# Hybrid encoder layer: from the second pair of row tiles on, the input is also loaded laid out by columns, and row factors are spread by two transposes and multiplied in place

## The chip, the core and the metric

The kernel runs on one core of one Trainium2 chip. The metric is the device time of one execution in microseconds (us). The engines are TensorE (PE; weight loads are shown apart as PEld), VectorE (DVE), ScalarE (ACT), GpSimd (POOL) and SyncE (SP), which issues most of the DMAs.

## The reference

One encoder layer is applied to two sequences (s = 0, 1) of 1024 rows by 1024 columns, all in float32. The part that matters here is the beginning:

```python
def rmsnorm(x, g):
    xf = x.astype(jnp.float32)
    y = xf * lax.rsqrt(jnp.mean(xf * xf, axis=-1, keepdims=True) + EPS)
    return (y * g.astype(jnp.float32)).astype(x.dtype)
...
    h = rmsnorm(x, g_mix) * (1.0 + sc1) + sh1
    z = h @ w_in
    q_lat, kv_lat, k_pe, f_in = z[..., :o1], z[..., o1:o2], z[..., o2:o3], z[..., o3:]
    y_mla = mla_group(q_lat, kv_lat, k_pe, g_q_lat, w_uq, g_kv_lat, w_ukv)
    y_four = fourier_group(f_in, w_four)
    mix = jnp.concatenate([y_mla, y_four], axis=-1) @ w_out
    x = x + ga1 * mix
    ...
```

Each row of x is divided by its root mean square (the row factor r), each column is scaled by g_mix (1 + sc1) and shifted by sh1, and the result is multiplied by w_in. Attention, a Fourier mixing, an output projection and a SwiGLU feed-forward follow; the change does not touch them.

## The kernel before

The first stage works on eight pairs of row tiles, four to a sequence; `pairs[k]` is (s, j), and the two tiles u = 0, 1 of pair k are 128 rows each, one from the first half of the sequence and one from the second. Matmuls that must be exact use a high and a low part of each operand: `split` makes the high part on ACT (line 62) and the rest on DVE (line 63), and `mm3` issues three matmuls (lines 78 to 80).

For pair k these steps exist:

- `x_load(k)` loads the two tiles, 128 rows by 1024 columns each, into two of four buffers `xt` (two DMAs on SP, line 356).
- `norm(k)` squares the rows on ACT with the sum beside it (line 366), makes r with six small POOL instructions in `rstd` (lines 103 to 110; the same helper also serves the projected latents), and multiplies the rows by r in place on DVE (line 369).
- `flip(k, g)`, for g = 0 to 3, transposes four blocks of 128 x 128 on PE into one PSUM bank (line 382); ACT scales and shifts them by column into `hf`, which holds the columns on partitions (line 385), and `split` makes `hh` and `hl` of them.
- `zproj(k, u)` projects one tile (24 matmuls of 448 columns with `wz`), squares the projected latents on ACT (lines 409, 410), gets their factors from POOL, scales on DVE (lines 421, 422) and writes `kv` by DMA (line 427). `latents(k, u)` transposes the scaled latents on PE (line 436), splits them (`lh`, `ll`) and writes them by DMA (line 441).
- `evenodd(k, i)` adds (i = 0) or subtracts (i = 1) the two tiles of `hf` on POOL (line 396) and splits the result; `fourier_in(k, i)` multiplies it by `wcs` (24 matmuls of 280 or 256 columns).

`pair(k)` strings them together, with the flips of pair k+1 and the norm of pair k+2 in between. A generator `extras` puts other work at three places of a pair: eight blocks of modulation products (`mod_mm`, line 217, four matmuls each, whose 1 MB weights go through two buffers `wada`, line 208), and later products with `lw` (line 311). In pair 0 four matmuls of line 252 stand there. A scheduler then orders the instructions of each engine by its own estimate; on the chip each engine runs its list in that order and waits at semaphores. PSUM has eight banks, all handed out in turn by `bank()`. Pair 7 runs in the next stage's pool, and after it the Fourier sums, attention and feed-forward follow.

Before the first pair, modulation and weight preparation share buffers with the stage: the tag `hf` serves for two weight loads before `hf` of pair 0 is made.

Of the kernel before, what the change touches and what calls it, by code (L numbers as in the profile page):

```python
# [12 lines left out]
F32 = mybir.dt.float32  # L13
# [3 lines left out]
ALU = mybir.AluOpType  # L17
# [4 lines left out]
P = 128  # L22
D = 1024
N = 1024
NC = D // P
# [27 lines left out]
def hybrid_encoder_kernel(ctx: ExitStack, tc: tile.TileContext, a: dict):  # L53
    nc = tc.nc
# [31 lines left out]
    ident = const.tile([P, P], F32, name="ident")  # L86
# [9 lines left out]
    def rstd(ms, n, rest=None):  # L96

        v = tiny.tile([P, 2], F32, name="rs_v")[:, :n]
        y = tiny.tile([P, 2], F32, name="rs_y")[:, :n]
        w = tiny.tile([P, 2], F32, name="rs_w")[:, :n]  # L100
        r = tiny.tile([P, 2], F32, name="rs_r")[:, :n]
        if rest is None:
            nc.gpsimd.tensor_scalar(out=v, in0=ms, scalar1=EPS, scalar2=None, op0=ALU.add)
        else:
            nc.gpsimd.tensor_tensor(out=v, in0=ms, in1=rest, op=ALU.add)
        nc.gpsimd.tensor_tensor(out=y, in0=v, in1=mhalf[:, :n], op=ALU.pow)  # L106
        nc.gpsimd.tensor_tensor(out=w, in0=y, in1=y, op=ALU.mult)
        nc.gpsimd.tensor_tensor(out=w, in0=w, in1=v, op=ALU.mult)
        nc.gpsimd.tensor_scalar(out=w, in0=w, scalar1=-0.5, scalar2=1.5, op0=ALU.mult, op1=ALU.add)
        here["p"] = nc.gpsimd.tensor_tensor(out=r, in0=w, in1=y, op=ALU.mult).ins  # L110
        return r
# [52 lines left out]
    with ExitStack() as st:  # L164
        p1b = st.enter_context(ExitStack())
        w2 = p1b.enter_context(tc.tile_pool(name="p1b", bufs=1, side="right", reuse_waits="tile"))
# [3 lines left out]
        def bank():  # L170
            return pp.tile([P, 512], F32, tag="b", name="bank")

        def xtile():
            return w2.tile([P, D], F32, tag="x", name="xt", bufs=4)

        def stile(name):
            return w.tile([P, 512], F32, tag="sk", name=name, bufs=3)
# [152 lines left out]
        def wz_split(i, t):  # L330
            for b in range(0, 4, 2):
                split(wz_h[:, i + b : i + b + 2, :], wz_l[:, i + b : i + b + 2, :], t[:, b : b + 2, :])
# [17 lines left out]
        st1 = {}  # L350

        def x_load(k):
            s, j = pairs[k]
            st1["x", k] = [xtile() for _ in range(2)]
            for u in range(2):
                nc.sync.dma_start(st1["x", k][u], xs[s][rows(j, u), :])

        def norm(k):
            if ("x", k) not in st1:
                x_load(k)  # L360
            ms = tiny.tile([P, 2], F32, name="ms")
            xt = st1["x", k]
            for u in range(2):
                t = xt[u]
                jk = w.tile([P, D], BF16, tag="junk", name="junk", bufs=1)
                nc.scalar.activation(jk, t, AF.Square, scale=1.0 / 32.0, accum_out=ms[:, u : u + 1])
            r = rstd(ms, 2)
            for u in range(2):
                nc.vector.tensor_scalar(out=xt[u], in0=xt[u], scalar1=r[:, u : u + 1], scalar2=None, op0=ALU.mult)

        def flip(k, g):
            s, j = pairs[k]
            if g == 0:
                st1["hf", k] = w2.tile([P, NC, 2, P], F32, tag="hf", name="hf", bufs=1)
                st1["hh", k] = w.tile([P, NC, 2, P], F32R, tag=f"hh{k % 2}", name="hh")
                st1["hl", k] = w.tile([P, NC, 2, P], F32R, tag=f"hl{k % 2}", name="hl")
            hf, xt = st1["hf", k], st1["x", k]
            pt = bank().rearrange("p (c u t) -> p c u t", c=2, u=2)
            for c in range(2):
                for u in range(2):  # L380
                    cc = 2 * g + c
                    nc.tensor.transpose(pt[:, c, u, :], xt[u][:, cc * P : (cc + 1) * P], ident)
            for c in range(2):
                cc = 2 * g + c
                nc.scalar.activation(hf[:, cc], pt[:, c], AF.Identity, bias=sh1[s][:, cc : cc + 1], scale=s1[s][:, cc : cc + 1])
            gs = slice(2 * g, 2 * g + 2)
            split(st1["hh", k][:, gs], st1["hl", k][:, gs], hf[:, gs])

        def evenodd(k, i):
            hf = st1["hf", k] if i == 0 else st1.pop(("hf", k))  # L390
            f = w.tile([P, NC, P], F32, tag="eo", name="eo", bufs=1)
            fh = w.tile([P, NC, P], F32R, tag=f"eoh{i}", name="eoh", bufs=1)
            fl = w.tile([P, NC, P], F32R, tag=f"eol{i}", name="eol", bufs=1)
            for g in range(2):
                gs = slice(4 * g, 4 * g + 4)
                nc.gpsimd.tensor_tensor(out=f[:, gs], in0=hf[:, gs, 0, :], in1=hf[:, gs, 1, :], op=(ALU.add, ALU.subtract)[i])
                split(fh[:, gs], fl[:, gs], f[:, gs])
            st1["eo", k, i] = (fh, fl)
# [74 lines left out]
                nc.sync.dma_start(zo[1], zo[0][2:3, :])  # L473

        def wide(tag, shape=(P, 4, 512)):
            return (w2 if tag == "hf" else w).tile(list(shape), F32, tag=tag, name="wide")

        cols0 = [(0, 2048)]
        fq = fold_loads()
# [35 lines left out]
        for g in range(4):  # L515
            flip(0, g)
        wz_split(4, wz1)
        norm(1)
        nc.sync.dma_start(ropec, a["ropec"])
        nc.sync.dma_start(ropes, a["ropes"])  # L520
# [1 line left out]
            prep_wcs(i, wf[i // 4])  # L522
        zproj(0, 0)
        evenodd(0, 0)
        evenodd(0, 1)
        nk = len(pairs)
        more = extras()

        def pair(k, also=None):
            if k + 2 < nk:  # L530
                x_load(k + 2)
            if also is not None:
                also(0)
            if k > 0:
                zproj(k, 0)
            if also is not None:
                with tc.issue_after(here["sq"]):
                    also(1)
            if k + 1 < nk:
                flip(k + 1, 0)  # L540
                flip(k + 1, 1)
            next(more, None)
            zproj(k, 1)
            if k < nk - 1:
                latents(k, 0)
            if k + 1 < nk:
                flip(k + 1, 2)
                flip(k + 1, 3)
            if k + 2 < nk:
                norm(k + 2)  # L550
            next(more, None)
            fourier_in(k, 0)
            if k > 0:
                if k == nk - 1:
                    latents(k, 0)
                latents(k, 1)
            if k + 1 < nk:
                evenodd(k + 1, 0)
            next(more, None)
            fourier_in(k, 1)  # L560
            if k == 0:
                latents(k, 1)
            if k + 1 < nk:
                evenodd(k + 1, 1)

        for k in range(nk - 1):
            pair(k)
# [422 lines left out]
    with ExitStack() as st:  # L990
# [105 lines left out]
        for k in range(nit + 4):  # L1096
# [7 lines left out]
            if k < nit:  # L1104
                s, b, h, u = items[k]
# [623 lines left out]
def _layout(i):  # L1729
    slots = _slots()  # L1730
    sq = {k: np.asarray(v)[0] for k, v in i.items() if k != "g_final"}
    c = np.stack([sq["c_prompt"], sq["c_sample"]])
    w_in, w_uq, w_ukv, w4 = sq["w_in"], sq["w_uq"], sq["w_ukv"], sq["w_four"]
    uq = w_uq.reshape(QL, HEADS, NOPE + ROPE)
    ukv = w_ukv.reshape(KVL, HEADS, NOPE + VD)
    rev = (GD - np.arange(GD)) % GD
    w4t = np.stack([w4, w4[:, rev, :]], 1).transpose(0, 3, 1, 2).reshape(4, P, 2, GD).transpose(1, 0, 2, 3)
    b = sq["b_ada"]
    bga = np.zeros((P, 512), b.dtype)
    for s in range(2):  # L1740
        for j, o in enumerate((2 * D, 2 * D + 512, 5 * D, 5 * D + 512)):
            bga[32 * j + s] = b[o : o + 512]
    wgu = np.stack([sq["w_gate"], sq["w_up"]]).reshape(2, NC, P, NF, P).transpose(0, 3, 2, 1, 4)
    r = {
        "x0": sq["x_prompt"][slots], "x1": sq["x_sample"][slots],
        "cT": c.reshape(2, NC, P).transpose(2, 1, 0),
        "w_ada": sq["w_ada"], "bT": b.reshape(48, P).T, "bga": bga,
        "gT": np.stack([sq["g_mix"], sq["g_ffn"]]).reshape(2, NC, P).transpose(2, 0, 1),
        "wz": w_in[:, :DZ].reshape(NC, P, DZ).transpose(1, 0, 2),
        "wfT": w_in[:, DZ:].T.reshape(4, P, D).transpose(1, 0, 2),  # L1750
        "wuqT": uq[:, :, :NOPE].transpose(2, 1, 0),
        "wpe": uq[:, :, NOPE:].reshape(2, P, HEADS * ROPE).transpose(1, 0, 2),
        "wukT": ukv[:, :, :NOPE].transpose(2, 1, 0),
        "wuvT": ukv[:, :, NOPE:].transpose(2, 1, 0),
        "gq": np.concatenate([sq["g_q_lat"].reshape(2, P).T, sq["g_kv_lat"].reshape(KVL, 1)], 1), "gkvr": sq["g_kv_lat"],
        "w4": w4t, "w_out": sq["w_out"], "wgu": wgu, "w_down": sq["w_down"], "g_final": np.asarray(i["g_final"]),
    }
    return {k: np.ascontiguousarray(v) for k, v in r.items()}
# [19 lines left out]
```

## Time and profile before

| | before |
|---|---|
| median of 3 runs | 2047.81 us (2044.94 to 2049.38) |
| the profiled execution | 2042.28 us |
| its span, first to last instruction | 2040.5 us |
| mean granted TensorE clock | 0.992 |
| busy: PE, PEld, DVE, ACT, POOL | 97%, 80%, 69%, 44%, 41% |
| DMA moved | 370.30 MB, mean 181 GB/s |

Times in the rows are those of the one profiled execution, counted from its first instruction. Matmuls overlap, and the end of each is modelled, so the time that a group of matmuls holds PE is read from its start to the start of the next group. The share in brackets behind an instruction, where there is one, is the engine's idle time in front of it and what ended it.

### The profile page before, as it was taken

How to read it: one execution, taken by the hardware profiler on the slowest of the kernel's cores; microseconds unless marked ns; L12 is line 12 of the kernel's file. 1: busy time of each engine (PE TensorE's matmuls, PEld its weight loads, DVE VectorE, ACT ScalarE, POOL GpSimd, SP SyncE). 2: the span in 40 equal slices, each digit the busy share in tenths (PEclk: the TensorE clock that was granted, in tenths of full speed). 3: DMA queues.
4: the chain of work that ended last, by engine and by line, in shares of the span. 5: the costliest groups of instructions: out<-in, count | busy, mean ns of one | idle time of the engine just before them, and what ended most of it. 6: DMA issues, size and time to landing. Idle time of an engine off the chain costs nothing.

```text
span 2040.5 us, 27843 instructions
## 1 busy us (share of the span) xinstructions
PE 1982.0 (97%) x9610; PEld 1626.2 (80%) x9610; DVE 1407.8 (69%) x2082; ACT 897.3 (44%) x1745; POOL 835.7 (41%) x1026
## 2 busy tenths in 40 slices
PE   5999999999999999999999999999999999999997
PEld 2788877888888877888888888877788888888876
DVE  2667757766677669878777676677756666667674
ACT  2656635555465554333333365453333333336451
POOL 1455213111313317879779410332654454410142
PEclk7999999999999999999999999999999999999999
DMA  9685694544643475545655587674422322358662
GB/s 369 204 269 187 217 338 136 130 103 99 165 115 121 127 276 198 191 166 200 198 163 196 174 305 251 214 236 144 141 104 103 106 101 103 107 183 275 227 229 85
DMA packets 182505, 370.30 MB, mean 181 GB/s; under 512 B 18972, under 2 KB 58396, under 8 KB 179292
## 3 DMA queue, kind: packets, MB, share of 16 engines
q1 hardware_dynamic: 163228, 308.88, 45.2%
q0 software_dynamic: 19136, 59.65, 9.7%
q8 instruction: 75, 1.23, 0.2%
q14 instruction: 66, 0.54, 0.1%
HBM read 256.46 MB, written 120.39 MB: 185 GB/s over the span
## 4 chain that ended last, share of the span: by engine, by line
PE 54%; DVE 2%; DMA 2%; POOL 1%; issue 1%; ACT 1%; SPq 0%; DVEq 0%; ACTq 0%; POOLq 0%
PE bank L78 18%; PE bank L79 18%; PE bank L80 18%; DVE wl L63 1%; DMA draw<-s_d 1%; DMA draw<-t_d 1%; DMA val<-x_d 1%; DVE val L138 0%; ACT wh L62 0%; POOL val L138 0%; DVE val L1577 0%; DMA rgu<-in_wgu_dram 0%; POOL rs_y L106 0%; SPq L1537 0%; DVE val L135 0%
## 5 line engine op out<-in xcount | busy, mean ns | idle before, releaser
L78 PE MATMUL bank<-H,wh 128*128 128x512 f32 x1224 | 477.2, 390 | 6.5 <-DVE val L138 6.0
L80 PE MATMUL bank<-H,wl 128*128 128x512 f32 x1224 | 476.4, 389 | 0.2
L79 PE MATMUL bank<-H,wh 128*128 128x512 f32 x1224 | 476.2, 389 | 0.0
L138 DVE TENSOR_TENSOR val<-bank,val 128x512 f32<-128x512 f32 x244 | 166.7, 688 | 160.6 <-PE bank L80 156.3
L78 PEld LDWEIGHTS bank<-H,wh 128*128 128x128 f32 x1224 | 229.7, 188 | 56.8 <-DVE val L138 6.6
L80 PEld LDWEIGHTS bank<-H,wl 128*128 128x128 f32 x1224 | 229.7, 188 | 49.6 <-DVE wl L63 1.4
L79 PEld LDWEIGHTS bank<-H,wh 128*128 128x128 f32 x1224 | 229.8, 188 | 47.4
L63 DVE TENSOR_TENSOR wl<-draw,wh 128x512 fp32r<-128x512 f32 x286 | 201.4, 738 | 86.8 <-ACT wh L62 86.4
L62 ACT CAST wh<-draw 128x512 fp32r<-128x512 f32 x286 | 169.0, 620 | 158.5 <-PE bank L79 93.1
L79 PE MATMUL bank<-wl,wh 128*128 128x512 f32 x572 | 223.9, 391 | 2.7 <-DVE wl L63 2.7
L138 POOL TENSOR_TENSOR val<-val 128x512 f32<-128x512 f32 x58 | 84.4, 1462 | 343.4 <-DVE val L1551 187.0
L80 PE MATMUL bank<-wh,wl 128*128 128x512 f32 x572 | 222.7, 389 | 0.0
L78 PE MATMUL bank<-wh 128*128 128x512 f32 x572 | 222.6, 389 | 0.0
L62 ACT CAST wh<-rgu 128x512 fp32r<-128x512 f32 x171 | 106.3, 623 | 249.9 <-PE bank L79 195.4
L63 DVE TENSOR_TENSOR wl<-val,wh 128x512 fp32r<-128x512 f32 x133 | 145.2, 1093 | 72.1 <-ACT wh L62 71.8
L63 DVE TENSOR_TENSOR wl<-rgu,wh 128x512 fp32r<-128x512 f32 x171 | 168.0, 983 | 7.0 <-ACT wh L62 7.0
L62 ACT CAST wh<-val 128x512 fp32r<-128x512 f32 x133 | 82.3, 622 | 179.9 <-PE bank L79 154.1
L135 POOL TENSOR_TENSOR val<-rgu 128x512 f32<-128x512 f32 x80 | 112.8, 1411 | 96.7 <-DMA rgu<-in_wgu_dram 93.0
L79 PEld LDWEIGHTS bank<-wl,wh 128*128 128x128 f32 x572 | 107.3, 188 | 28.9 <-DVE wl L63 6.6
L78 PEld LDWEIGHTS bank<-wh 128*128 128x128 f32 x572 | 107.4, 188 | 22.4
L80 PEld LDWEIGHTS bank<-wh,wl 128*128 128x128 f32 x572 | 107.4, 188 | 22.0
L135 POOL TENSOR_TENSOR val<-val 128x512 f32<-128x512 f32 x89 | 119.3, 1359 | 1.3
(385 smaller groups left out, 3901.2 us busy)
## 6 DMA issues: line engine op xcount, KB each, us to landing
rgu<-in_wgu_dram SPq DMA_DIRECT2D x86, 512.0 KB
draw<-s_d SPq DMA_DIRECT2D x143, 256.0 KB
s_d<-val POOLq DMA_DIRECT2D x88, 256.0 KB, 3.8
draw<-t_d SPq DMA_DIRECT2D x88, 256.0 KB
s_d<-val SPq DMA_DIRECT2D x66, 256.0 KB
draw<-in_w_down_dram SPq DMA_DIRECT2D x55, 256.0 KB
wada<-in_w_ada_dram SPq DMA_DIRECT2D x13, 1024.0 KB
xt<-in_x_dram SPq DMA_DIRECT2D x16, 512.0 KB
```

The lines of the kernel that those rows point to most:

```text
L62: here["a"] = nc.scalar.copy(hi, src).ins
L63: here["v"] = nc.vector.tensor_tensor(out=lo, in0=src, in1=rd(hi), op=ALU.subtract).ins
L78: nc.tensor.matmul(out, lh, rh, start=first, stop=False, skip_group_check=cont)
L79: nc.tensor.matmul(out, lh, rl, start=False, stop=False, skip_group_check=cont)
L80: nc.tensor.matmul(out, ll, rh, start=False, stop=last, skip_group_check=cont)
L135: return eng.tensor_tensor(out=out, in0=x, in1=y, op=ALU.subtract).ins
L138: return eng.tensor_tensor(out=out, in0=x, in1=y, op=ALU.add).ins
```

## The change

The tiles are also stored in HBM a second time, transposed: `xT0` and `xT1` hold, for each j, the columns on partitions, as `hf` does (8 KB in a row on each of 128 partitions). From pair 1 on, `xT_load(k)` loads 1 MB of this straight into `hf`, which now has two buffers; `xt` has two in place of four. `norm(k)` stops at r. A new step `scale_cols(k)` transposes r, broadcast along the free axis, once for each tile, so that each partition of a PSUM bank holds the factors of all 256 rows, and DVE multiplies `hf` by it in place, in two instructions. `flip(k, g)` then has no transposes: ACT reads `hf` and writes `hf`. Pair 0 stays as it was.

```diff
@@ xtile
-            return w2.tile([P, D], F32, tag="x", name="xt", bufs=4)
+            return w2.tile([P, D], F32, tag="x", name="xt", bufs=2)
@@ behind x_load
+        def xT_load(k):
+            s, j = pairs[k]
+            st1["hf", k] = w2.tile([P, NC, 2, P], F32, tag="hf", name="hf", bufs=2)
+            nc.sync.dma_start(st1["hf", k], a[f"xT{s}"][j])
+
@@ norm
             r = rstd(ms, 2)
+            if k > 0:
+                st1["r", k] = r
+                return
             for u in range(2):
                 nc.vector.tensor_scalar(out=xt[u], in0=xt[u], scalar1=r[:, u : u + 1], scalar2=None, op0=ALU.mult)
+
+        def scale_cols(k):
+            hf, r = st1["hf", k], st1.pop(("r", k))
+            pr = bank()[:, :256].rearrange("p (u t) -> p u t", u=2)
+            for u in range(2):
+                nc.tensor.transpose(pr[:, u, :], r[:, u : u + 1].broadcast_to([P, P]), ident)
+            for g in range(2):
+                gs = slice(4 * g, 4 * g + 4)
+                nc.vector.tensor_tensor(out=hf[:, gs], in0=hf[:, gs], in1=pr.unsqueeze(1).broadcast_to([P, 4, 2, P]), op=ALU.mult)
@@ flip
             if g == 0:
-                st1["hf", k] = w2.tile([P, NC, 2, P], F32, tag="hf", name="hf", bufs=1)
+                if k == 0:
+                    st1["hf", k] = w2.tile([P, NC, 2, P], F32, tag="hf", name="hf", bufs=2)
...
-            pt = bank().rearrange("p (c u t) -> p c u t", c=2, u=2)
-            for c in range(2):
-                for u in range(2):
-                    cc = 2 * g + c
-                    nc.tensor.transpose(pt[:, c, u, :], xt[u][:, cc * P : (cc + 1) * P], ident)
+            if k > 0:
+                pt = hf[:, 2 * g : 2 * g + 2]
+            else:
+                pt = bank().rearrange("p (c u t) -> p c u t", c=2, u=2)
+                for c in range(2):
+                    for u in range(2):
+                        cc = 2 * g + c
+                        nc.tensor.transpose(pt[:, c, u, :], xt[u][:, cc * P : (cc + 1) * P], ident)
@@ before pair 0
         wz_split(4, wz1)
+        xT_load(1)
         norm(1)
...
         evenodd(0, 0)
+        scale_cols(1)
         evenodd(0, 1)
@@ pair(k)
             if k + 2 < nk:
                 x_load(k + 2)
+                xT_load(k + 2)
...
             if k + 1 < nk:
                 evenodd(k + 1, 1)
+            if k + 2 < nk:
+                scale_cols(k + 2)
@@ _layout
+        **{f"xT{s}": x[slots].reshape(2, 4, P, NC, P).transpose(1, 4, 3, 0, 2)
+           for s, x in enumerate((sq["x_prompt"], sq["x_sample"]))},
```

In the changed kernel the squares of `norm` have line 371, the multiply of pair 0 line 377, the transposes of r line 383, the multiply of `hf` line 386, the transposes of pair 0 line 403, the scaling line 406, the copies to `kv` go out at line 448 and the latents at line 462.

PE, behind the second projection of pair 0 (the last two rows of that projection come first; `lat` are the scaled latents, line 252 is the work with `wo2`). Before:

```order
L79 MATMUL bank<-wz_l,hh 128x448
L80 MATMUL bank<-wz_h,hl 128x448
L436 MATMUL bank<-ident,lat 128x128 x4
L382 MATMUL bank<-ident,xt 128x128 x8
L252 MATMUL bank<-wada,wuvT 128x512 x2
L78 MATMUL bank<-wcs_h,eoh 128x280
```

Now:

```order
L79 MATMUL bank<-wz_l,hh 128x448
L80 MATMUL bank<-wz_h,hl 128x448
L457 MATMUL bank<-ident,lat 128x128 x4
L252 MATMUL bank<-wada,wuvT 128x512 x2
L78 MATMUL bank<-wcs_h,eoh 128x280
```

The eight transposes of two flips are gone. At the end of pair 0, between the second Fourier product and the first projection of pair 1, PE has now (`rs_r` is r of pair 2; before, the fourth row was not there):

```order
L79 MATMUL bank<-wcs_l,eoh 128x256
L80 MATMUL bank<-wcs_h,eol 128x256
L457 MATMUL bank<-ident,lat 128x128 x4
L383 MATMUL bank<-ident,rs_r 128x128 x2
L78 MATMUL bank<-wz_h,hh 128x448
```

The transposes of r stand ahead of the projections of the next pair, here and in pairs 1 to 5.

ACT, in pair 1 behind its second projection (`mz` are the squares of the latents, `ms` those of pair 3's rows). Before:

```order
L409 ACTIVATE junk,mz<-bank 128x256
L410 ACTIVATE junk,mz<-bank 128x128
L62 CAST lh<-bank 128x512
L385 ACTIVATE hf<-bank,sh_0_77,s_0_75 128x256 x3
L62 CAST hh<-hf 128x512
L62 CAST kv<-lat 128x128
L385 ACTIVATE hf<-bank,sh_0_77,s_0_75 128x256
L366 ACTIVATE junk,ms<-xt 128x1024
L62 CAST hh<-hf 128x512
L366 ACTIVATE junk,ms<-xt 128x1024
```

Now:

```order
L430 ACTIVATE junk,mz<-bank 128x256
L431 ACTIVATE junk,mz<-bank 128x128
L62 CAST lh<-bank 128x512
L62 CAST hh<-hf 128x512
L371 ACTIVATE junk,ms<-xt 128x1024
L62 CAST kv<-lat 128x128
L371 ACTIVATE junk,ms<-xt 128x1024
```

The scalings of `hf` have moved ahead of the projection's end, and the first square stands ahead of the copy of `kv`.

SP, the load of the second block of modulation weights (the row with `wada` x2). Before:

```order
L427 DMA ckv_d_96<-kv 128x128
L441 DMA lat_d_93<-ll 512x1x128
L427 DMA ckv_d_97<-kv 128x128
L255 DMA wo_d<-so 128x512 x2
L208 DMA wada<-in_w_ada_dram 128x1024 x2
L441 DMA lat_d_92<-lh 512x1x128
```

Now:

```order
L462 DMA lat_d_92<-lh 512x1x128
L462 DMA lat_d_93<-ll 512x1x128
L356 DMA xt<-in_x_dram 128x1024
L361 DMA hf<-in_xT_dram 128x2048
L448 DMA ckv_d_96<-kv 128x128
L448 DMA ckv_d_97<-kv 128x128
L208 DMA wada<-in_w_ada_dram 128x1024 x2
```

The block's load was issued behind the writes of pair 0; now it stands behind the loads of pair 3 and the write of pair 1's first `kv`.

4 lines of the change are left out of this document (3 added, 1 removed).

## The prediction

> **What bounds the kernel now.** I read the page first, then busy time in stretches cut at the pairs of row tiles, then TensorE (PE) in order of time, and last the waits.
>
> ```profile
> PE 1982.0 (97%) x9610; PEld 1626.2 (80%) x9610; DVE 1407.8 (69%) x2082; ACT 897.3 (44%) x1745; POOL 835.7 (41%) x1026
> ```
>
> PE is busy nearly all the time, so only PE's own work, or a wait that PE takes over, moves the end. The change lies in the first stage, which ends near 232 us. Each stretch below runs from one pair's first projection to the next pair's (pair 0 from the end of its own); its columns are busy time of PE, weight loads, DVE, ACT and POOL, the granted clock, the DMA share and GB/s.
>
> ```profile
> 62.30:82.50 20.20, 17.25 (x104) 14.16 (x103) 14.38 (x40) 12.12 (x34) 10.96 (x20) 1.00 0.29 96
> 82.50:104.80 22.30, 22.27 (x147) 18.03 (x146) 14.50 (x30) 15.30 (x39) 12.62 (x28) 1.00 0.78 239
> 104.80:126.60 21.80, 21.80 (x146) 18.05 (x145) 11.66 (x26) 13.76 (x34) 12.56 (x31) 1.00 0.85 276
> 126.60:147.40 20.80, 20.80 (x139) 18.05 (x138) 13.35 (x28) 13.47 (x33) 11.60 (x24) 1.00 0.76 252
> ```
>
> From pair 1 on PE is full (22.27 of 22.30 us); DVE, ACT and POOL have 6 to 10 us of room in a pair. Pair 0 is different: PE stands idle for 3 us of 20.2. And in pairs 1 to 3 the DMA engines are already three quarters to 85% busy.
>
> **What is removed.** Pair 1 on PE, in order of time (start, length, name; the next row's start is what counts, because matmuls overlap):
>
> ```profile
> 87.57 1.03 PE L382 MATMUL bank<-ident,xt 128*128 128x128 f32 x8
> 88.54 1.06 PE L217 MATMUL bank<-wada,scT 128*32 128x512 f32 x8
> ...
> 94.67 0.69 PE L436 MATMUL bank<-ident,lat 128*128 128x128 f32 x4
> 95.20 1.04 PE L382 MATMUL bank<-ident,xt 128*128 128x128 f32 x8
> 96.16 1.06 PE L217 MATMUL bank<-wada,scT 128*32 128x512 f32 x8
> 97.16 0.40 PE L78 MATMUL bank<-wcs_h,eoh 128*128 128x280 f32 x1
> ...
> 100.38 0.60 PE L436 MATMUL bank<-ident,lat 128*128 128x128 f32 x4
> 100.91 1.06 PE L217 MATMUL bank<-wada,scT 128*32 128x512 f32 x8
> 101.90 0.39 PE L78 MATMUL bank<-wcs_h,eoh 128*128 128x256 f32 x1
> ...
> 104.84 0.37 PE L78 MATMUL bank<-wz_h,hh 128*128 128x448 f32 x1
> ```
>
> A block of eight transposes holds PE for 0.97 us here (87.57 to 88.54, 95.20 to 96.16). There are 14 such blocks for pairs 1 to 7; the shortest take 0.79, as the first and the last do:
>
> ```profile
> 62.32 1.03 PE L382 MATMUL bank<-ident,xt 128*128 128x128 f32 x8
> 63.11 0.45 PE L78 MATMUL bank<-wz_h,hh 128*128 128x448 f32 x1
> ...
> 207.05 1.04 PE L382 MATMUL bank<-ident,xt 128*128 128x128 f32 x8
> 207.84 0.38 PE L78 MATMUL bank<-wcs_h,eoh 128*128 128x280 f32 x1
> ```
>
> Eight of the 14 take about 0.97, one 0.87 and five 0.79: 12.6 us in all, 0.11 us a transpose. The Trainium skill ("VectorE: DVE Perf Modes", The three transpose paths) gives 390 ns for one 128x128 transpose on TensorE, for bf16; by that the 112 transposes would be 43.7 us. The trace does not agree for transposes in a row, and I use the 12.6.
>
> **What is added on PE.** Two transposes of the row factors per pair, seven times. Nearest row: four transposes in a row hold PE for 0.53 us (94.67 to 95.20, 100.38 to 100.91), so two take 0.2 to 0.3; I take 0.25, that is 1.75 us. Net on PE: 10.8 us less.
>
> **DVE and ACT.** The two multiplies by row factors (0.75 us each) become two over 1024 columns from PSUM. The second and third row read PSUM with 512 and 256 columns (the fourth is for pair 0, below):
>
> ```profile
> L369 DVE TENSOR_SCALAR xt<-xt,rs_r 128x1024 f32<-128x1024 f32 x12 | 8.5, 751 | 11.1 <-POOL rs_r L110 11.1
> L63 DVE TENSOR_TENSOR ll<-bank,lh 128x512 fp32r<-128x512 f32 x14 | 9.6, 683 | 0.1
> L342 DVE TENSOR_TENSOR wcs_l<-bank,wcs_h 128x256 fp32r<-128x256 f32 x6 | 2.4, 420 | 0.0
> L62 ACT CAST hh<-hf 128x512 fp32r<-128x512 f32 x28 | 17.6, 628 | 0.2
> ```
>
> 683 less 420 for 256 columns is 1.03 ns a column, so 1024 columns take 683 + 512 x 1.03 = 1.21 us. DVE gets 0.9 us more in a pair, inside its 6 to 10 us of room: nothing on the path. ACT's scaling reads SBUF in place of PSUM; no row shows that form. The cast of hh from SBUF takes 628 ns for 512 columns, that of the latents from PSUM 0.59 us (below): 0.05 us each way, ACT has room, and I take nothing.
>
> **The new wait.** Before, PE needed the row factor r of pair k+2 only in pair k+1, through the scaled rows. Now the two transposes of r stand at the end of pair k, and every projection of pair k+1 stands behind them. Here is when r is ready in pair 1 (for pair 3):
>
> ```profile
> 96.22 0.38 ACT L409 ACTIVATE junk<-bank 128x256 bf16<-128x256 f32 x1
> ...
> 96.84 0.59 ACT L62 CAST lh<-bank 128x512 fp32r<-128x512 f32 x1
> 97.30 1.50 ACT L385 ACTIVATE hf<-bank,sh,s 128x256 f32<-128x256 f32 x3
> ...
> 100.39 0.30 ACT L62 CAST kv<-lat 128x128 fp32r<-128x128 f32 x1 [1.08 <-DVE lat L422]
> ...
> 101.06 1.05 ACT L366 ACTIVATE junk<-xt 128x1024 bf16<-128x1024 f32 x1
> 102.61 1.05 ACT L366 ACTIVATE junk<-xt 128x1024 bf16<-128x1024 f32 x1
> 103.84 0.22 POOL L103 TENSOR_SCALAR rs_v<-ms 128x2 f32<-128x2 f32 x1 [1.30 <-ACT junk L366]
> 105.75 0.20 POOL L110 TENSOR_TENSOR rs_r<-rs_w,rs_y 128x2 f32<-128x2 f32 x1
> ```
>
> r is ready at 105.95, and PE begins the next pair at 104.84: with the order of before, PE would already wait 1.1 us, and with 1.7 us less work in front, 2.8. But the order on ACT moves too: the first square stands ahead of the copy of kv, and the scalings that ran between (0.5 us each) are done earlier. By these rows: the second projection ends at T; ACT squares the projected latents (96.22 to 96.84: 0.6) and copies kv 3.55 later (96.84 to 100.39), the time of POOL's chain and DVE; the second square follows 0.25 later and takes 1.25; POOL's chain for r takes 2.1 (103.84 to 105.95). That is T + 7.75. PE gets there at T + 0.53 + 3.2 + 0.53 + 2.9 = T + 7.2, and at T + 8.2 with one block of modulation products between. So PE waits 0 to 0.6, and where ACT or POOL run late, up to the 2.8. I take 0.7 in each of pairs 1 to 5: 3.5 us.
>
> **Pair 0.** Its two stalls of PE are waits for PSUM banks that ACT and DVE had not read (72.70 and 79.24):
>
> ```profile
> 66.20 0.48 DVE L421 TENSOR_SCALAR lat<-bank,rs_r 128x256 f32<-128x256 f32 x1 [1.34 <-POOL rs_r L110]
> ...
> 72.70 0.39 PE L78 MATMUL bank<-wcs_h,eoh 128*128 128x280 f32 x1 [1.51 <-ACT hf L385]
> ...
> 79.24 0.39 PE L78 MATMUL bank<-wcs_h,eoh 128*128 128x256 f32 x1 [1.44 <-DVE lat L422]
> ...
> 82.54 0.45 PE L78 MATMUL bank<-wz_h,hh 128*128 128x448 f32 x1
> ```
>
> The scaled rows' transposes no longer take four banks in a pair, so both can go: 2.95 us. PE would come to the transposes of r near 78. But that r waits for ACT. DVE scales the first projected latents at 66.20 and then multiplies: 66.2 + 0.8 + 1.2 = 68.2. From there ACT's row holds eight scalings (4.0), four casts (4 x 0.63 = 2.5), the squares and the copy of the latents (0.6 + 0.5), the copy of kv (0.3, and by my estimate 0.3 of waiting for it) and the two squares (2.8): 79.2. POOL's chain ends at 81.3. PE starts pair 1 at about 81.6, not 82.54; 0.9 us stays of the 1.66 - 0.25 + 2.95 = 4.4, so 3.5 go back.
>
> **DMA.** Seven loads of 1 MB more, on the same SP queue, and the rows' own load moves later, since only two buffers are left. The room in pairs 1 to 3 is the second point at issue. The highest rates of the trace:
>
> ```profile
> 0.00:40.00 40.00, 17.81 (x76) 6.86 (x80) 8.68 (x19) 5.58 (x8) 6.39 (x20) 0.76 0.92 362
> 240.00:280.00 40.00, 38.82 (x204) 24.51 (x203) 21.75 (x38) 16.75 (x34) 1.05 (x2) 1.00 0.96 352
> ```
>
> 362 GB/s at a share of 0.92 is 393 at full share, so 1.05 MB cost 2.7 us of all engines. Pairs 1 to 3 hold 0.80 x 21.6 = 17.2 us of it on average; 19.9 of a pair of 20.3 us is 98%. The modulation weights share that queue, and the order now puts each of their loads behind the writes of kv, where they stood ahead of them. PE's modulation products will sometimes be in front of their data: between 0 and 2 us for each of the seven blocks after the first; I take 1 us in all, since before no such wait shows (in the rows of pair 1 above none of the three blocks has an idle time in front).
>
> **The sum.** 10.8 + 2.95 - 3.5 (pair 0) - 3.5 (pairs 1 to 5) - 1.0 = 5.75, say 5.5 us less. Behind the first stage every engine's instructions stand as before, with PE full, so the gain is passed on. The profiled execution took 2042.28 us, its span being 2040.5; it lies 5.5 below the median of the three runs, 2047.81. So 2036.8 for the one, 2042.3 for a median.
>
> **Rivals.**
> 1. The norm chain takes it all (0.26): the squares wait on ACT behind the kv copy as they did, PE waits 1.5 in each of pairs 1 to 5, 4 us more. For it: 105.95 against 104.84. Against: ACT's new order. Time: 1.5 less, 2046.3.
> 2. Slower: the DMA queue fills in pairs 1 to 3 (0.20). A pair then moves 5.5 + 1.05 = 6.6 MB and cannot be shorter than that takes. It decides below 6.6 MB / 20.3 us = 323 GB/s. If these small writes sustain no more than 255, the mean of the three rows, a pair takes 25.7 us and not 21.6: 12.5 us more in three pairs, less the 0.9 and some 4 of the others: 7 slower, 2055. For it: 0.85 in pair 2. Against: 0.80 at 255 extrapolates to 320, just at the point.
> 3. The clock falls (0.04). After an idle stretch the same transposes ran slower:
>
> ```profile
> 39.24 1.93 PE L217 MATMUL bank<-wide,scT 128*32 128x512 f32 x8 [5.87 <-DMA wide<-in_w_ada_dram]
> ...
> 45.45 3.09 PE L382 MATMUL bank<-ident,xt 128*128 128x128 f32 x16
> 48.38 7.31 PE L337 MATMUL bank<-c,wada 128*128 128x128 f32 x64
> ```
>
> 16 transposes from 45.45 to 48.38 are 0.18 us each against 0.10 at 62.32. If PE idles as long at the end of pair 0, it loses those 3 us and some 3 more at the low rate: no gain, 2048. The Trainium skill ("TensorE: Matmul & The Clock Gate", Part 1) says that an idle window of about 3.4 us halves the clock; the 5.87 us here agree with it.
>
> **How the numbers follow.** The forecast has 0.50. A measurement of this kernel tells about 0.2% (4.1 us) from no change: faster means under 2043.7, slower over 2051.9. Of the forecast's 0.50, 0.05 falls within. Faster 0.45; same 0.05 + 0.26 + 0.01 + 0.02 = 0.34; slower 0.19 + 0.02 = 0.21. The range: the low end is all of 10.8 and half of pair 0's 2.95, 12.3 less, 2035.5; the high end reaches into rival 2, 2052.5, and leaves out the rest of it and little else.
>
> **What would show it.** Right: the transposes of r wait under 1 us in pairs 1 to 5 and 2 to 4 us in pair 0; pairs 1 to 6 are 0.7 to 1.5 us shorter each; the first stage ends 5 to 6 us earlier, and everything behind it moves by as much. Wrong: waits of PE at the transposes of r of 2 us and more in every pair (rival 1); waits of PE for modulation weights with a DMA share over 0.95 in pairs 1 to 3 (rival 2); a granted clock under 1.00 behind 82 us (rival 3); or a row of eight removed transposes that gives back less than 0.8 us.

## The result and the profile after

The changed kernel takes 2062.54 us (median of 6 runs, 2060.82 to 2066.72) against 2046.88 for the kernel before beside it (median of 5): ratio 1.0077, 95% interval 1.0064 to 1.0089. A sixth run of the kernel before took 3203.12 us and is left out. The change is about 16 us slower, where 5.5 us faster was forecast, and 10 us above the end of the range. The profiled execution took 2060.82 us with a span of 2059.0, 18.5 more than before.

The page's line on busy time and the stretches cut at the pairs, as in the prediction (pair 0 from the end of its own first projection; then the pairs 1 to 3, and pair 6, whose row for before stands last):

```profile
PE 1989.0 (97%) x9512; PEld 1622.2 (79%) x9512; DVE 1431.0 (70%) x2082; ACT 900.7 (44%) x1745; POOL 844.8 (41%) x1026
63.28:83.81 20.53, 15.97 (x93) 13.31 (x93) 14.21 (x29) 13.12 (x30) 13.59 (x27) 0.94 0.69 224
83.81:107.74 23.93, 22.33 (x124) 18.16 (x123) 14.78 (x28) 13.51 (x32) 11.69 (x27) 0.91 0.72 226
107.74:132.69 24.95, 24.02 (x133) 16.69 (x132) 14.00 (x26) 14.02 (x33) 14.23 (x28) 1.00 0.75 257
132.69:157.20 24.51, 24.04 (x133) 16.71 (x132) 13.46 (x26) 13.90 (x33) 11.79 (x26) 1.00 0.79 271
210.83:235.81 24.98, 20.64 (x107) 19.16 (x105) 15.90 (x30) 10.70 (x27) 9.09 (x19) 0.80 0.42 137
```

```profile
195.59:214.31 18.72, 18.37 (x123) 17.40 (x122) 15.01 (x31) 11.33 (x29) 10.60 (x20) 1.00 0.38 123
```

PE executes fewer instructions (98 records less) and is busy longer. Pairs 2 and 3 lost 3 to 4 us each while PE was still nearly full (24.02 of 24.95 us), so there its work grew; pair 6 lost 6 us at a granted clock of 0.80 with PE partly idle. Pair 5, whose rows are not shown, lost 5.5 (27.8 us, before 22.3). And the DMA share in pairs 1 to 3 did not rise (0.72 to 0.79, before 0.76 to 0.85), although each pair has 1 MB more to load.

The first stage ended at 231.85 us before and at 252.60 after (start of the first Fourier sum): 20.7 us. That the whole span grew by 18.5 only is no gain of the later stages: what follows the first stage took 1806 to 1814 us in the traces of all 18 kernels of this case. PE's time in the first stage, from the wait in front of its first projection on, each group counted from its start to the next group's start without the idle time (us; the third column is the experiment with the column loads on GpSimd's queue, further down):

| PE, first stage | before | after | loads on GpSimd |
|---|---|---|---|
| transposes of rows / of r | 12.55 | 1.25 | 1.20 |
| projections | 78.43 | 84.43 | 81.39 |
| Fourier products | 52.07 | 56.08 | 52.86 |
| modulation products | 7.97 | 14.75 | 9.47 |
| other (latents, `lw`, line 252) | 18.68 | 19.20 | 18.74 |
| waits | 6.46 | 21.56 | 8.78 |
| sum | 176.2 | 197.3 | 172.4 |

So 11.3 us were saved (forecast 10.8), and 32 lost: 15.1 by waits, 6.8 at the modulation products, 10 at projections and Fourier products, whose number is the same. PE in order of time shows all three (start, length, name, and the idle time in front):

```profile
83.47 0.69 PE L383 MATMUL bank<-ident,rs_r 128*128 128x128 f32 x2 [4.56 <-DVE so L254]
...
84.70 0.57 PE L80 MATMUL bank<-wz_h,hl 128*128 128x448 f32 x1
...
88.38 0.36 PE L78 MATMUL bank<-wz_h,hh 128*128 128x448 f32 x1
88.58 0.36 PE L79 MATMUL bank<-wz_l,hh 128*128 128x448 f32 x1
...
101.46 1.05 PE L217 MATMUL bank<-wada,scT 128*32 128x512 f32 x4 [1.60 <-DMA wada<-in_w_ada_dram]
102.44 0.40 PE L79 MATMUL bank<-wcs_l,eoh 128*128 128x280 f32 x1
...
103.28 1.05 PE L217 MATMUL bank<-wada,scT 128*32 128x512 f32 x4
104.26 0.66 PE L457 MATMUL bank<-ident,lat 128*128 128x128 f32 x4
...
210.64 0.43 PE L383 MATMUL bank<-ident,rs_r 128*128 128x128 f32 x2 [3.06 <-POOL rs_r L110]
...
226.61 1.23 PE L457 MATMUL bank<-ident,lat 128*128 128x128 f32 x4 [4.33 <-DVE lat L442]
```

First, idle time and what follows it. PE waits 4.56 us for r(2) (POOL ends it at 83.42; the profile names a DVE instruction that ended about then), and behind the wait the projections come every 0.37 us until 88.38, then every 0.20: 2.1 us more for the 24 of them. The 48 projections behind 210.83 (11.45 us, in pair 5 10.14) and the 24 Fourier products behind 227.50 (5.04, in pair 5 3.20) show the same: 5.3 us in all, about half of the 10. The granted clock was 0.50 in these stretches: from 81.47 to 88.30 us, from 211.18 to 214.59 and from 224.83 to 231.66. The Trainium skill ("TensorE: Matmul & The Clock Gate", Part 1) has the clock halved after an idle window of about 3.4 us. This row agrees with it in part: a wait of 4.56 us did it, but the clock fell 2.6 us after PE had stopped (78.91).

Of the other half, some 3 us lie in pairs 1 to 3, where halves of modulation products stand among the projections and the Fourier products: the 48 projections took 10.59 us in pair 2 and in pair 3 (before 9.75), the Fourier products of pairs 1 to 3 6.49 to 6.69 (before 6.13 to 6.16). That the halves cause this was not tried by itself.

Second, the products. A whole modulation block, two halves in a row in the trace, held PE for 1.00 us before (96.16 to 97.16 in the prediction's rows); here the scheduler has put matmuls of another kind between the halves of seven of the eight blocks, and each half holds PE for 0.98 us (101.46 to 102.44, 103.28 to 104.26). The four matmuls of a block write 32 partitions each, and by these times they run beside one another; two of them take as long as four. That agrees with the Trainium skill ("TensorEngine Tiling (Array Packing)", Key Properties), which says that the tiles of a divided array can execute in parallel.

Third, waits for weights in pairs 1 to 3 (1.60 us here, 2.81 in all), for `lw` in pair 4 (1.63) and for the latents in pairs 5 and 6 (1.67 and 4.33).

### The profile page after: what moved, and what is told of

Its sections match the earlier page's. It is cut to its first block, busy times and chain, and to the rows that moved or that the text cites. A ratio compares the mean times of both kernels' runs of the same rounds, so it can differ in the third digit from the quotient of the medians.

```text
span 2059.0 us, 27663 instructions
## 1 busy us (share of the span) xinstructions
PE 1989.0 (97%) x9512; PEld 1622.2 (79%) x9512; DVE 1431.0 (70%) x2082; ACT 900.7 (44%) x1745; POOL 844.8 (41%) x1026
## 3 DMA queue, kind: packets, MB, share of 16 engines
q8 instruction: 74, 1.21, 0.3%
## 4 chain that ended last, share of the span: by engine, by line
PE 53%; DMA 2%; DVE 2%; POOL 1%; issue 1%; SPq 0%; ACT 0%; DVEq 0%; ACTq 0%; POOLq 0%
PE bank L79 18%; PE bank L78 18%; PE bank L80 18%; DMA draw<-t_d 1%; DVE wl L63 1%; DMA val<-x_d 1%; POOL val L138 1%; DVE val L138 0%; ACT wh L62 0%; DVE val L1605 0%; POOL rs_y L106 0%; DMA draw<-in_w_down_dram 0%; DMA draw<-s_d 0%; SPq L1564 0%; DMA rgu<-in_wgu_dram 0%
## 5 line engine op out<-in xcount | busy, mean ns | idle before, releaser
L63 DVE TENSOR_TENSOR wl<-val,wh 128x512 fp32r<-128x512 f32 x133 | 151.4, 1140 | 61.8 <-ACT wh L62 61.5
L63 DVE TENSOR_TENSOR wl<-rgu,wh 128x512 fp32r<-128x512 f32 x171 | 176.4, 1032 | 5.6 <-ACT wh L62 5.5
```

What stands on the lines that cost most here:

```text
L63: here["v"] = nc.vector.tensor_tensor(out=lo, in0=src, in1=rd(hi), op=ALU.subtract).ins
```

## The experiments

**The r transposes, the cut products, the loads.** In `e1_r_late` the r transposes stand behind the next pair's first projection:

```diff
@@ pair(k), behind the first zproj
+            if k > 0 and k + 1 < nk:
+                scale_cols(k + 1)
@@ pair(k), at the end
-            if k + 2 < nk:
-                scale_cols(k + 2)
```

> The changed kernel with scale_cols(k+2) called one step later, after the first z projection of the next pair, so that the two r transposes and the multiplies stand behind 24 projections on TensorE; nothing else is edited. Theory R (the r transposes hold TensorE until the norm chain is done): the waits at 83.47 and 210.64 (4.56 and 3.06 us) and the slow stretches behind them (projections held 7.06 instead of 4.92 us, 11.45 instead of about 9.8) go: 9 to 12 us faster than the changed kernel, about 2051 to 2054 us. Theory M (the modulation products are cut in halves): they stay cut in this kernel, so no more than 3 us faster, 2059 to 2063. Theory O (the latents' chain comes late because ScalarE, VectorE and GpSimd now take the next pair's work first): the multiplies come later and push the flips, so 0 to 4 us slower or faster, with waits for lat still 4 us or more.

Measured: 2063.01 us, ratio to before 1.0077 (1.0061 to 1.0093), the same as the changed kernel. The waits at the transposes are gone, and PE waits elsewhere as long; its rows:

```profile
84.89 0.43 PE L383 MATMUL bank<-ident,rs_r 128*128 128x128 f32 x2
...
99.84 1.92 PE L217 MATMUL bank<-wada,scT 128*32 128x512 f32 x4 [4.80 <-DMA wada<-in_w_ada_dram]
...
226.42 1.35 PE L457 MATMUL bank<-ident,lat 128*128 128x128 f32 x4 [6.19 <-DVE lat L442]
```

Theory R falls: what PE gained by coming earlier it spent waiting for the modulation weights. Something behind the transposes was late by itself.

In `e2_one_load` each block's weights come in one load, and the order has the products whole:

```diff
-                    nxt = mod_load(c + 1, cols1, wada_tile())
+                    nxt = mod_load1(c + 1, wada_tile())   # one DMA for both column ranges
```

> The changed kernel with the two 0.5 MB loads of each w_ada block of the second modulation made one 1 MB load; with that the order has all eight products as whole blocks of four matmuls instead of seven cut into halves; the r transposes stay where they are. Theory M (a half block holds TensorE as long as a whole one, 0.98 us): the modulation products hold about 8 us instead of 14.75, and 5 to 9 us go, 2053 to 2057 us. Theory R: TensorE's waits at the r transposes stay (4 to 5 us and 3 us), so the saving is M's part and not more. If the halves had cost nothing: 2061 to 2064.

Measured: 2055.87 us, ratio 1.0047 (1.0033 to 1.0061): 6.7 us less. The groups of instructions by line, for 60 to 160 us, of after and of this run (count, busy time, mean ns, idle time in front):

```profile
L217 PE MATMUL bank<-wada,scT 128*32 128x512 f32 x64 | 15.8, 605 | 2.8 <-DMA wada<-in_w_ada_dram 2.8
```

```profile
L222 PE MATMUL bank<-wada,scT 128*32 128x512 f32 x64 | 8.5, 605 | 2.7 <-DMA wada<-in_w_ada_dram 2.7
```

The same 64 records of 605 ns cover 15.8 us in halves and 8.5 whole. Theory M holds for this part; the waits stayed.

`e4_loads` is the kernel before with two row buffers, and the column loads into a buffer that nothing reads:

```diff
-            return w2.tile([P, D], F32, tag="x", name="xt", bufs=4)
+            return w2.tile([P, D], F32, tag="x", name="xt", bufs=2)
@@ pair(k)
                 x_load(k + 2)
+                xT_load(k + 2)   # into a tile ht of its own
```

> The kernel before (rows transposed on TensorE, factors multiplied in rows) with two row buffers instead of four and with the seven 1 MB loads of the column layout added into a buffer that nothing reads. Theory L (7.3 MB more through the DMA queue and later x loads delay the products' weights): 5 us or more slower than the kernel before, 2052 to 2058 us, with waits for wada in pairs 1 to 3. Theories R, M and O (the time goes to TensorE's order and to the chain that it now waits for): within 3 us of the kernel before, 2045 to 2050.

Measured: 2058.0 us, ratio 1.0056 (1.0041 to 1.007): theory L's number. But its waits were not those of theory L: PE waited 0.8 us for weights, and 9.1 for the multiply by row factors and for latents. So the buffers alone were tried next.

`e6_norm_early` calls `norm(k + 2)` ahead of `flip(k + 1, 0)`:

> The changed kernel with norm(k+2) called before the flips of pair k+1 instead of after them: the squares and the reciprocal root of pair k+2 stand a half pair earlier on ScalarE and GpSimd, while TensorE's order is nearly the same, the r transposes ahead of the projections and the products in halves. Theory R: r is there before TensorE comes to the transposes in pair 0 (wait 4.56 falls below 1 us) and in pair 5 (3.06 falls below 1): 6 to 11 us faster than the changed kernel, 2052 to 2057. Theory O: the squares push the latents' chain back, so what is won at the transposes is lost at the latents' waits: within 3 us of the changed kernel, 2060 to 2065.

Measured: 2067.77 us, ratio 1.0101 (1.0083 to 1.0119): 5 us slower than the changed kernel. No wait at the transposes above 1.0 us, and 9.45 us for the latents at 215.33. Neither theory had a slower run; it speaks against R once more.

**Bytes, buffers or the place in the queue.** `e3_x2` has only the buffers:

> The kernel before with two row buffers instead of four and nothing else: the control of the run with the added loads, which came out 12 us above the kernel before. If the added bytes cost that: within 3 us of the kernel before, 2043 to 2049. If the missing buffers cost it (x(k+2) can be loaded only when the flips of pair k are done): 6 us or more above the kernel before, 2052 to 2058, with TensorE waiting for the row factors' multiply at the flips as it did with the loads.

Measured: 2057.0 us, ratio 1.0043 (1.003 to 1.0055), not to be told from the run with the loads. So the loads' 7.3 MB by themselves cost at most a few us; the missing buffers cost the kernel *before* some 9. Whether they cost the changed kernel anything is another question, since it needs the rows only for their squares.

`e5_no_rows` leaves out the row loads of pairs 2 to 7 and keeps the column loads:

```diff
+            if k > 1:
+                st1["x", k] = st1["x", 1]
+                return
```

> The changed kernel without the row loads of pairs 2 to 7 (the squares of these pairs read the rows of pair 1 again), so that the first stage moves 6 MB less; its order has the products whole, in the places of the kernel before, and the r transposes ahead of the projections. If the bytes set the pace of the first stage: 12 to 18 us faster than the changed kernel, 2045 to 2051. If the chain from squares to r to flips and latents sets it: only the 5 to 9 us of the cut products go, 2053 to 2058, and the waits at the r transposes and latents stay at 8 us or more.

Measured: 2040.28 us, ratio 0.9959 (0.9946 to 0.9971): 22 us below the changed kernel. Loads taken off do it; this run leaves open whether by bytes or by their place. The next one decides.

`e8_pool_queue` moves the column loads of pairs 2 to 7 to GpSimd's queue:

```diff
-            nc.sync.dma_start(st1["hf", k], a[f"xT{s}"][j])
+            (nc.sync if k == 1 else nc.gpsimd).dma_start(st1["hf", k], a[f"xT{s}"][j])
```

> The changed kernel with the column loads of pairs 2 to 7 issued by GpSimd instead of SyncE, where they don't stand ahead of or behind the products' weights and the writes; the same bytes, and the order has the products whole. If the place in SyncE's queue costs the time: 12 to 18 us faster than the changed kernel, 2045 to 2051. If the bytes cost it: only the cut products' 5 to 9 us go, 2053 to 2058, with waits for wada in pairs 1 to 3. If the issue work on GpSimd delays its reciprocal roots: no more than 3 us faster, or slower.

Measured: 2040.96 us, ratio 0.9958 (0.9944 to 0.9971): all of the loss is gone, with the same bytes and the same two buffers, and the kernel is faster than before. Its stretches for the pairs 2 and 3:

```profile
106.98:128.30 21.32, 21.32 (x134) 16.55 (x131) 14.16 (x26) 13.94 (x34) 14.07 (x29) 1.00 0.99 330
128.30:148.03 19.73, 19.73 (x126) 16.40 (x123) 14.36 (x28) 13.95 (x33) 10.73 (x27) 1.00 0.92 321
```

The DMA engines are busy for 0.99 and 0.92 of the time, and PE shows no idle time. It still lost some 1.5 us to late weights in these two pairs: the second half of one product in each waited for its load, so that the two blocks held PE for 1.81 and 1.68 us and not for 1.00. In pair 2 (PEld loads the weights of the next matmuls):

```profile
118.67 0.14 PEld L217 LDWEIGHTS bank<-wada,scT 128*32 128x32 f32 x4 [0.17 <-issue]
119.50 0.14 PEld L217 LDWEIGHTS bank<-wada,scT 128*32 128x32 f32 x4 [0.69 <-DMA wada<-in_w_ada_dram]
```

So a full DMA share cost little. The difference is in what SyncE issues, and when; in after (the weights of the second block are the last line):

```profile
85.97 0.63 SPq L356 DMA_DIRECT2D xt<-in_x_dram  x1
86.71 1.01 SPq L361 DMA_DIRECT2D hf<-in_xT_dram  x1
95.11 1.81 SPq L448 DMA_DIRECT2D ckv_d<-kv  x2
97.02 0.86 SPq L208 DMA_DIRECT2D wada<-in_w_ada_dram  x2
```

and in this run:

```profile
85.98 6.32 SPq L208 DMA_DIRECT2D wada<-in_w_ada_dram  x3
95.11 1.80 SPq L448 DMA_DIRECT2D ckv_d<-kv  x2
96.96 0.43 SPq L208 DMA_DIRECT2D wada<-in_w_ada_dram  x1
```

The write of kv goes out at 95.11 in both, when ACT has made kv. In after, the scheduler has the weights of the second block behind that write, and they leave at 97.02; with the column loads out of the list they stand in front of it, at 85.98. That is eleven microseconds, and in after PE has come to the product by 99.9.

`e5_no_rows` had the column loads on SyncE, in one queue with the weights, and PE waited for no weights there either. In its order too they stand early: the second block's leave at 80.67 and the first half of the third block's at 92.29, in front of kv:

```profile
80.67 1.19 SPq L208 DMA_DIRECT2D wada<-in_w_ada_dram  x2
...
87.12 0.34 SPq L364 DMA_DIRECT2D hf<-in_xT_dram  x1
92.29 0.34 SPq L208 DMA_DIRECT2D wada<-in_w_ada_dram  x1
95.40 1.79 SPq L451 DMA_DIRECT2D ckv_d<-kv  x2
```

`e7_pool_late` is the same with the r transposes late, as in `e1_r_late`:

> The run with the column loads on GpSimd, and on top of it the r transposes and multiplies behind the first z projection of the next pair. With the products whole and the loads off SyncE, theory R expects the waits at the transposes (4.6 and 3.1 us and the slow clock behind them) to turn into time: 5 to 10 us faster than with the loads on GpSimd alone. If the pace is set by bytes or by the latents' chain: within 3 us of it.

Measured: 2044.98 us, ratio 0.9981 (0.9969 to 0.9993), 4 us above `e8_pool_queue`. The 5.04 us wait for r(2) has then shrunk to 0.25, and PE waits 1.40, 2.93 and 0.93 us for weights instead.

**Controls, and the weights in place of the columns.** `b1_rows_pool` is the kernel before with its row loads of pairs 2 to 7 on GpSimd's queue:

> The kernel before with the row loads of pairs 2 to 7 issued by GpSimd instead of SyncE, all else as it was: the control for the run with the column loads on GpSimd, which came out 7 us below the kernel before. If those 7 us come from the shorter work of TensorE with columns: within 3 us of the kernel before, 2045 to 2051. If they come from relieving SyncE's queue alone: 2038 to 2044.

Measured: 2044.75 us, ratio 0.9991 (0.9981 to 1.0002). Relieving SyncE brings the kernel before little; the rest of `e8_pool_queue`'s gain comes with the columns.

`b2_x2_rows_pool` adds two row buffers to that:

> The kernel before with two row buffers (which cost 9 us) and its row loads of pairs 2 to 7 on GpSimd's queue. If two buffers cost time because a load that waits for its buffer holds up what stands behind it on SyncE: most of the 9 us go, 2046 to 2051. If they cost time because the rows themselves come too late for norm and flips: it stays at 2054 to 2060.

Measured: 2066.38 us, ratio 1.0103 (1.0084 to 1.0123): in the layout by rows two buffers cost time because the rows themselves come too late, whatever queue brings them (PE waits up to 4.79 us for the multiply by r). That a load held up what stands behind it on SyncE, the other reading of `e3_x2`, falls. Neither expectation had 2066 us: GpSimd's queue makes it some 9 us worse than `e3_x2`, and why was not followed.

`e10_wada_pool` leaves the column loads on SyncE and moves the weights of the second modulation to GpSimd's queue:

> The changed kernel with the weights of the second modulation issued by GpSimd and the column loads left on SyncE; the order has the products whole (one is cut by a transpose). If the cost of the change is that the weights and the column loads share SyncE's queue: 14 us or more faster than the changed kernel, 2040 to 2048. If the column loads themselves block what else is on SyncE (the row loads and the latents' writes): only the cut products and their waits go, 7 to 10 us, 2052 to 2056.

Measured: 2047.78 us, ratio 1.0008 (0.9999 to 1.0017): 15 us come back by separating the two kinds of loads the other way round, about 7 of which `e2_one_load` gave for whole products alone. The column loads on SyncE are therefore not what costs most, though 7 us above `e8_pool_queue` remain. Nor is it the sharing of one queue as such, since `e5_no_rows` shares it without loss. What `e5_no_rows`, `e8_pool_queue` and this kernel have in common is that the second block's weights leave early, ahead of the write of kv in pair 1: at 80.67 in `e5_no_rows`, 85.98 in `e8_pool_queue` and 82.33 here.

`e9_pool_norm2` adds to `e8_pool_queue` that `norm(2)`, in pair 0 alone, is called before the flips:

> The column loads on GpSimd, and norm(2) called before the flips of pair 1 instead of after them, in pair 0 alone. In the run with the column loads on GpSimd TensorE waits 5.04 us for r(2) at the end of pair 0, and the 24 projections behind it hold it 6.86 instead of 4.92 us. If that wait is time: 4 to 7 us faster than that run, 2034 to 2037 us. If what TensorE gains there is lost at the next transfer (the products' weights are the bound of pairs 1 to 3, DMA share 0.92 to 0.97): within 2 us of it, 2039 to 2043.

Measured: 2036.53 us, ratio 0.9955 (0.994 to 0.997). The wait at the transposes of r(2) is gone (they start at 77.52 with no idle time), 2.92 us of waiting for latents and 2.5 for weights come instead, and the first stage ends at 226.35 us and not 229.21. Of the ratios, 0.9955 and 0.9958, one cannot say that they differ. Both kernels beat the two of the comparison.

**Where the rest of the loss comes from.** With the products whole (`e2_one_load`) pairs 5 and 6 were still long. `f1_r_first` puts GpSimd's even and odd adds behind r(k+2) there:

> The changed kernel with one load for each block of the second modulation's weights (2055.87 us), and GpSimd's even and odd adds of pair k+1 put behind r(k+2) in its order; the column loads stay on SyncE. If the order on GpSimd is what makes r(7) late and with it VectorE's products and the latents of pair 6: the waits of 3.05 and 4.32 us and the slow clock behind them go, 7 to 12 us faster, 2044 to 2049. If r(7) is late because its squares are late (ScalarE), or the latents wait for something else: within 3 us of 2055.87, 2053 to 2059.

Measured: 2062.43 us, ratio 1.0088 (1.0074 to 1.0102). r(7) came in time (PE waits 0.20 us at 204.04), and the latents of pair 6 cost 6.99 us instead of 4.32. So an r(7) in time gained nothing.

`f5_last_pool` moves only the column loads of pairs 6 and 7 off SyncE, `f6_first_pool` only those of pairs 2 to 5:

> The changed kernel with one load for each block of the second modulation's weights, and only the column loads of pairs 6 and 7 on GpSimd's queue. If the loss in pairs 5 and 6 comes from these two loads' place on SyncE, among the writes of the row products: pairs 5 and 6 fall from 27.8 and 26.5 us to about 24.4 and 17.7, 9 to 12 us faster than 2055.87, 2044 to 2047. If it was handed down from the pairs before them: within 3 us of 2055.87.

> The changed kernel with the column loads of pairs 2 to 5 on GpSimd's queue and those of pairs 6 and 7 on SyncE's. The order has the products whole. If the cost is in two parts with a place each: the cut products' part goes, 7 to 10 us, and pairs 5 and 6 stay long, 2051 to 2056 us. If all comes from the earlier loads: as with all of them on GpSimd, 2039 to 2043.

Measured: `f5_last_pool` 2056.31 us, ratio 1.0055 (1.0042 to 1.0068), no gain over 2055.87; `f6_first_pool` 2044.9 us, ratio 0.9998 (0.9989 to 1.0007), 17.6 us below the changed kernel. Pair 6 in the first and in the second, from the end of pair 5's work (the first begins with 3.29 us of waiting for r(7)):

```profile
200.90:230.00 29.10, 21.07 (x106) 19.43 (x107) 17.80 (x33) 11.88 (x29) 11.30 (x26) 0.82 0.37 117
```

```profile
194.00:215.80 21.80, 18.37 (x109) 17.20 (x108) 15.82 (x32) 12.26 (x29) 9.84 (x20) 0.92 0.52 165
```

Most of the loss in pairs 5 and 6 is handed down from the loads of pairs 2 to 5. Not all of it is: `f6_first_pool` stays 4 us above `e8_pool_queue`, whose pair 6 is 4 us shorter (17.56 us from its first projection to pair 7's, in `f6_first_pool` 21.62). Neither of its two expectations, 2051 to 2056 and 2039 to 2043, has this time. SyncE's issues show a way, in after and in `e8_pool_queue`:

```profile
164.63 0.33 SPq L298 DMA_DIRECT2D ga_d<-modrow  x1
165.00 0.93 SPq L356 DMA_DIRECT2D xt<-in_x_dram  x2
166.03 0.38 SPq L361 DMA_DIRECT2D hf<-in_xT_dram  x1
167.41 3.13 SPq L448 DMA_DIRECT2D ckv_d<-kv  x2
170.65 1.73 SPq L305 DMA_DIRECT2D gah<-ga_d  x2
```

```profile
148.32 0.33 SPq L298 DMA_DIRECT2D ga_d<-modrow  x1
148.70 1.29 SPq L356 DMA_DIRECT2D xt<-in_x_dram  x2
151.43 0.81 SPq L305 DMA_DIRECT2D gah<-ga_d  x2
```

The row of the second modulation can be written only when its eighth product is done (153.75 to 156.6 on PE in after, 139.72 in `e8_pool_queue`). It leaves 16 us later, and the rows of pair 6 and the loads of `gah` stand behind it on SyncE. DVE's products with `gah` then fall into pair 6, where three groups of them (220.38, 222.83, 224.67) stand in front of the scaling of the latents for which PE waits (their factors were ready at 222.96):

```profile
220.38 1.28 DVE L315 TENSOR_TENSOR so<-bank,gah 128x512 f32<-128x512 f32 x2
...
224.67 1.28 DVE L315 TENSOR_TENSOR so<-bank,gah 128x512 f32<-128x512 f32 x2
226.07 0.48 DVE L442 TENSOR_SCALAR lat<-bank,rs_r 128x256 f32<-128x256 f32 x1
```

That the early loads hand most of the loss down is shown; that they do it by this way is read from the rows and was not tried by itself.

`f3_best` joins `e9_pool_norm2` with the rows on GpSimd too:

> The kernel with the column loads on GpSimd and norm(2) early (2036.53 us), and the row loads of pairs 2 to 7 on GpSimd's queue too. If what still waits for weights in pairs 1 and 2 (1.16 and 1.36 us) waits for SyncE's queue: 1 to 4 us faster, 2033 to 2036. If GpSimd's own queue is then too long for its roots and adds, or rows come too late there as they did in the kernel with two row buffers: 2038 or more.

Measured: 2042.56 us, ratio 0.9983 (0.9974 to 0.9992), 6 us above `e9_pool_norm2`. PE waits 3.90 us for latents at 97.99 and 2.43 for r(1) at 64.49. This fits a queue on GpSimd that has become too long, but the cause was not tried further.

## Why the prediction was wrong

- **The work removed and added on PE**: right. 12.55 us of transposes went and 1.25 came (forecast 12.6 and 1.75). The multiply takes 1.21 us (forecast 1.21) and is not on the path.
- **Pair 0**: right in its mechanism, too small. Both bank stalls went; r(2) was ready at 83.42, not 81.3, and PE stood idle for 4.56 us. The clock fell with it, rival 3's mechanism (0.04), which I had for an improbable one: pair 1 began at 83.81, not 81.6, and cost 2.1 more. Rival 3's sign came, a granted clock under 1.00 behind 82 us. Its own row showed less than I read from it: in the trace of before the granted clock was 0.50 all the way from 27.38 to 47.86 us, so it had fallen before the idle time of 5.87 us in front of 39.24. The wait for r(1) at 63.28 (1.56 us) I had not seen.
- **Pairs 1 to 5, 0.7 us each at the transposes of r**: wrong in place, and right in sum by luck: none in pairs 1 to 4 and 3.06 in pair 5, 3.5 forecast. And `e1_r_late` shows that these waits bound nothing: taken away, they came back elsewhere.
- **"I take 1 us in all" for the modulation products: the step that failed.** I saw the weights fall behind the writes of kv and priced only PE's direct wait, which measured 2.81 us. Left out were the cut blocks, in the order before the chip ran (6.8 us; 6.7 came back in `e2_one_load`), and what the late products hand on to pairs 5 and 6, which were 5.5 and 6.3 us longer than before (handed down for the most part, by `f6_first_pool`). With the column loads off SyncE and the weights early again, 2040.96 us were measured against the forecast's 2042.3. That this comes so close is in part luck: in `e8_pool_queue` PE waits 5.04 us for r(2) and the clock falls as well, 1.5 us go to late weights, nothing waits at the transposes of r in pairs 1 to 5, and in its one trace the first stage ends 2.6 us earlier than before, not 5 to 6.
- **Rival 2 (0.20, 2055 us)** had the side and the pairs, and not the reason: it made the bytes the limit and put the point at 323 GB/s. `e8_pool_queue` runs a pair at 330 and loses 0.8 us there. And rival 2's sign, a DMA share over 0.95 in pairs 1 to 3, did not come (0.72 to 0.79).
- **"The gain is passed on" behind the first stage**: right, as far as one trace of each can tell: 20.7 us at its end, 18.5 at the end of the span.

What stays open: `e8_pool_queue` changes the queue at run time and, with it, the order that the scheduler plans for every engine (the products whole, the weights ahead of kv). How much each does alone was not separated beyond the 6.7 us of the cut blocks. `e5_no_rows` speaks for the order, since it keeps the queue, but it also moves 6 MB less. No run keeps all loads on SyncE and only puts the weights ahead of kv.

## What to carry to other kernels

Price an added load not by its bytes but by its place: what stands behind it in the list of the engine that issues it, what that list waits for, and how the scheduler reorders the rest around it. When a wait vanishes and the time stays, look for the transfer that the freed engine now reaches first. Before the run, read the order for blocks that were whole and are now cut: here each cut of a product cost about 1 us.

## What was not expected of the hardware

- Four matmuls that write 32 partitions each hold PE for 1.00 us together, and two of them 0.98.
- An idle time of 3.06 us (at 210.64) was enough for a granted clock of 0.50 and projections 0.37 us apart from 211.42 to 214.41, while 3.05 us in `e2_one_load` (207.19) left the 48 projections behind it at 9.85 us. The Trainium skill's window of about 3.4 us ("TensorE: Matmul & The Clock Gate", Part 1) is not a sharp bound here.
- The DMA engines ran at a share of 0.99 and 330 GB/s through a whole pair, and PE lost 0.8 us of its 21.32 to a late load.
